# Norm blocks in pairs and a deferred attention epilogue in a hybrid mLSTM and attention block on eight cores

## The chip, the cores and the metric

The kernel runs on all eight cores of one Trainium2 chip, as one program. Two cores share one of the four sequences. A core has five engines that run side by side: PE multiplies matrices, ACT applies functions, DVE does elementwise work, POOL (GpSimd) and SP (here only issuing transfers) do little (busy shares of the kernel before, core 3: PE 69%, ACT 53%, DVE 36%, POOL 2%). They work from SBUF, the core's working memory; PE writes its products to PSUM, which this program uses as eight banks, 0 to 7. Reading a bank out is called an eviction. The metric is the device time of the slowest core, in microseconds (us), lower being better.

Executions of one kernel do not all agree: in some of them the cores of a die (one half of the chip, cores 0 to 3 or 4 to 7) show a lower granted TensorE clock, and the time is some per cent longer. The granted clock is the share of the full clock that the profile records; in these traces it is 0.5, 13/16 or 1 (2423, 588 and 3928 us on core 1 of the kernel before), and a mean of these is quoted for a stretch. Such executions are called slow and are not compared with fast ones. The medians of the kernel before lie between 6999 and 7117 us over this study, on different chips and with different shares of slow executions, so kernels are compared by ratios of fast runs to the kernel before on the same chip, and parts of a kernel by the traces.

## The reference, cut to what matters

One decoder block: a norm, two token mixers (an mLSTM and a differential attention) side by side on its result, their merge, a second norm and a gated feed-forward part.

```python
def rms_norm(x, g):
    xf = x.astype(jnp.float32)
    y = xf * lax.rsqrt(jnp.mean(xf * xf, axis=-1, keepdims=True) + RMS_EPS)
    return (y * g.astype(jnp.float32)).astype(x.dtype)
...
h = rms_norm(x, norm1_g[l]) * (1.0 + scale1) + shift1          # first norm
proj = h @ w_in[l]
...
p = jax.nn.softmax(logits, axis=-1)                            # two maps per head
wts = p[:, :, 0] - lam * p[:, :, 1]
ha = einsum(wts, v)                                            # shortened here
ha = rms_norm(ha, a_norm_g[l]...) * (1.0 - lam_init)           # the attention epilogue
y = sigmoid(g_m) * (hm @ w_branch_m[l]) + sigmoid(g_a) * (ha @ w_branch_a[l])
x = x + gate1 * (y @ w_out[l])
h2 = rms_norm(x, norm2_g[l]) * (1.0 + scale2) + shift2         # second norm
```

D_MODEL is 1024, the sequence has 8192 tokens, and there are 4 attention heads of width 128.

## The kernel before

A core works through 16 units of 512 tokens. Units 0 to 6 only build keys, values and the mLSTM state (first norm and projections). Units 7 to 15 are full: first norm, projections, attention with the mLSTM woven in, merge, second norm, feed-forward. That makes 16 first and 9 second norms, and 9 units with 4 attention heads. Unit 7 does one quarter of its queries only (32 items per head); units 8 to 15 have 74 to 130 items per head.

The program is written as a list of operations. Each goes to one engine's queue in the order in which it is emitted, and semaphores are derived from the buffers that it reads and writes. **An engine takes its queue in order**, so what is emitted first runs first on that engine. The traces show it: for ACT, the Square of the fourth norm block of unit 10 (kernel before, core 3) started at 3050.55, behind the third block's evictions, though all rows of x had landed by 3039.2 at the latest. A norm is four blocks of 128 tokens, each emitted from end to end:

```python
def norm_block(st, j, mult, shift, hdst, b_hdst, tagp):
    ...
    S.op("act", activation(out=junk, in_=xs[:, j, :], func=Square, accum_out=ss[:, 0:1]))
    S.op("act", activation(out=ss[:, 1:2], in_=ss[:, 0:1], func=Ln, bias=eps))
    S.op("act", activation(out=ss[:, 1:2], in_=ss[:, 1:2], func=Exp, scale=-0.5))
    S.op("dve", tensor_scalar(out=xn, in0=xs[:, j, :], scalar1=ss[:, 1:2], op0=mult))
    for half in range(2):
        pv = a PSUM bank
        ... 4 x S.op("pe", transpose(out=pv[:, cc], in_=xn[...]))
        ... 4 x S.op("act" if half == 0 else "dve", hdst = pv * mult + shift)   # the evictions
...
for j in range(4):
    norm_block(st, j, ...)
```

In attention an item is one key block for one or two query blocks: a score matmul into one of three PSUM banks (4 to 6, used as a ring), an exp on ACT, and the PV matmuls (the weights times the values), which run three items later into accumulators in banks 0 to 3. Every one or more items a step of the mLSTM (a Python generator, `mdrv`, with bank 7) is emitted between them. When a head's items are out, its epilogue follows on the spot:

```python
for h in range(4):
    for jq in range(4): memset(accs[jq])                        # DVE
    for idx in range(len(items) + LAG):
        if idx < len(items): emit_scores(items[idx], idx)       # PE, ACT
        if idx >= LAG: emit_pv(items[idx - LAG], idx - LAG)     # PE
        if gcount[0] % MSTEP == 0: next(mdrv, None)
    for jq in range(4):
        ... 5 small DVE operations: har[jq] = acc0/l0 - lam * acc1/l1, read from PSUM
    Square (ACT), tensor_reduce (DVE), Ln, Exp (ACT), 4 x scaling to haf (DVE)
    4 x transpose (PE) into score bank 4 + h % 3, copy to haT (DVE)
```

The softmax here doesn't subtract the row's maximum and nothing guards it: scores larger than these inputs give would overflow.

Of the kernel before, what the change touches and what calls it, by code (L numbers as in the profile page):

```python
# [188 lines left out]
def build_program(NCTX, NFULL, debug=False):  # L189
# [45 lines left out]
    with ExitStack() as top:  # L235
# [19 lines left out]
        def bfview(bank):  # L255
            return bank[:].bitcast(BF16)
# [192 lines left out]
        for u in range(NU):  # L449
# [3 lines left out]
            with ExitStack() as su:  # L453
# [23 lines left out]
                def norm_block(st, j, mult, shift, hdst, b_hdst, tagp):  # L477
# [4 lines left out]
                    if ck not in st.ncache:  # L482
# [4 lines left out]
                    S.op("act", lambda e: e.activation(out=junk[:], in_=xs[:, j, :], func=AF.Square, scale=1.0 / 32.0, accum_out=ss[:, 0:1]),  # L487
                         reads=[b_xs[j]], writes=[bl])
                    S.op("act", lambda e: e.activation(out=ss[:, 1:2], in_=ss[:, 0:1], func=AF.Ln, bias=epst[:, 0:1], scale=1.0), reads=[bl, CONST], writes=[bl])
                    S.op("act", lambda e: e.activation(out=ss[:, 1:2], in_=ss[:, 1:2], func=AF.Exp, scale=-0.5), reads=[bl], writes=[bl])  # L490
                    S.op("dve", lambda e: e.tensor_scalar(out=xn[:], in0=xs[:, j, :], scalar1=ss[:, 1:2], scalar2=None, op0=ALU.mult),
                         reads=[bl, b_xs[j]], writes=[b_xn])
                    for half in range(2):
                        pb, pbb = nbank()
                        pv = bfview(pb)[:, 0:512].rearrange("p (c t) -> p c t", c=4)
                        for cc in range(4):
                            c = half * 4 + cc
                            S.op("pe", lambda e: e.transpose(out=pv[:, cc, :], in_=xn[:, c * 128:(c + 1) * 128], identity=identb[:]),  # L498
                                 reads=[b_xn, cb[0]], writes=[pbb])
                        for cc in range(4):  # L500
# [4 lines left out]
                            else:  # L505
                                S.op("dve", lambda e: e.tensor_scalar(out=hdst[:, c, j * 128:(j + 1) * 128], in0=pv[:, cc, :], scalar1=mult[:, c:c + 1],
                                                                     scalar2=shift[:, c:c + 1], op0=ALU.mult, op1=ALU.add), reads=[pbb, CONST], writes=[b_hdst[1]])

                with ExitStack() as st:
# [13 lines left out]
                    for j in range(4):  # L523
                        norm_block(st, j, mult1, shift1, hT, (b_hT, b_hT2), "n1")
# [322 lines left out]
                if full:  # L847
                    with ExitStack() as st:
# [34 lines left out]

                        for h in range(4):
# [65 lines left out]
                            for jq in range(4):  # L950
                                ab, abb = accs[jq]
                                av = ab[:, 0:260].rearrange("p (m c) -> p m c", m=2)
                                S.op("dve", lambda e: e.tensor_scalar(out=rr[:, 2 * jq:2 * jq + 2], in0=av[:, :, 128], scalar1=1e-30, scalar2=None, op0=ALU.max), reads=[abb], writes=[b_a])  # L953
                                S.op("dve", lambda e: e.reciprocal(out=rr[:, 2 * jq:2 * jq + 2], in_=rr[:, 2 * jq:2 * jq + 2]), reads=[b_a], writes=[b_a])
                                S.op("dve", lambda e: e.tensor_tensor(out=rr[:, 2 * jq + 1:2 * jq + 2], in0=rr[:, 2 * jq + 1:2 * jq + 2], in1=neglam[:], op=ALU.mult),
                                     reads=[b_a, CONST], writes=[b_a])
                                S.op("dve", lambda e: e.tensor_scalar(out=har[:, jq, :], in0=av[:, 0, 0:128], scalar1=rr[:, 2 * jq:2 * jq + 1], scalar2=None, op0=ALU.mult),
                                     reads=[abb, b_a], writes=[b_a])
                                S.op("dve", lambda e: e.scalar_tensor_tensor(out=har[:, jq, :], in0=av[:, 1, 0:128], scalar=rr[:, 2 * jq + 1:2 * jq + 2], in1=har[:, jq, :],
                                                                            op0=ALU.mult, op1=ALU.add), reads=[abb, b_a], writes=[b_a])  # L960
                            S.op("act", lambda e: e.activation(out=hsq[:], in_=har[:], func=AF.Square, scale=1.0 / math.sqrt(128.0)), reads=[b_a], writes=[b_a])
                            S.op("dve", lambda e: e.tensor_reduce(out=hss[:, 0:4], in_=hsq[:], axis=AX.X, op=ALU.add), reads=[b_a], writes=[b_a])
                            S.op("act", lambda e: e.activation(out=hss[:, 4:8], in_=hss[:, 0:4], func=AF.Ln, bias=epst[:, 0:1], scale=1.0), reads=[b_a, CONST], writes=[b_a])
                            S.op("act", lambda e: e.activation(out=hss[:, 4:8], in_=hss[:, 4:8], func=AF.Exp, scale=-0.5), reads=[b_a], writes=[b_a])
                            for jq in range(4):
                                S.op("dve", lambda e: e.scalar_tensor_tensor(out=haf[:, jq, :], in0=har[:, jq, :], scalar=hss[:, 4 + jq:5 + jq], in1=ang[:, h * 128:(h + 1) * 128],  # L966
                                                                            op0=ALU.mult, op1=ALU.mult), reads=[b_a, CONST] + cb, writes=[b_a])
                            tb, tbb = banks[4 + h % 3], bbufs[4 + h % 3]
                            tv = bfview(tb)[:, 0:512].rearrange("p (j t) -> p j t", j=4)
                            for jq in range(4):  # L970
                                S.op("pe", lambda e: e.transpose(out=tv[:, jq, :], in_=haf[:, jq, :], identity=identb[:]), reads=[b_a, cb[0]], writes=[tbb])  # L971
# [310 lines left out]
```

## Time and profile before

The times are medians; the stage rows are read from the trace of each kernel's profiled execution, as the mean over the eight cores of the sum over all units. A stage begins and ends at the first or last matmul (or Square) that belongs to it, so the rows of one core add up to its span.

| | before |
|---|---|
| median of the first 6 runs | 6998.55 us |
| profiled run: slowest core, and all | 7048.9 us, 6953.4 to 7048.9 us |
| preamble (weights recast) | 557.3 us |
| first norms (16) | 336.9 us |
| projections | 1433.1 us |
| attention with mLSTM (9 units) | 2503.0 us |
| merge | 592.4 us |
| second norms (9) | 177.5 us |
| feed-forward | 1324.7 us |
| tail of the units | 72.9 us |

### The profile page before, as it was taken

Reading aid. Unit: us, or ns where it says so; the run is one execution under the profiler, and the core shown is the slowest. Engines: PE = TensorE matmul, PEld = TensorE weight load, DVE = VectorE, ACT = ScalarE, POOL = GpSimd, SP = SyncE. Lnnn points to the kernel's source line nnn. Section 1 sums busy time; section 2 is a strip of 40 time slices with the busy share of each in tenths; the row PEclk is TensorE's granted clock in tenths of the full one; section 3 lists DMA queues with packets and bytes.
Section 4 is the critical chain, followed back from the end, with each engine's and each line's share of the span. In section 5 each row is a group of like instructions: output and inputs, shape, how many; then the busy total and the mean of one; then the engine's idle time right before and its main releaser. Section 6 shows DMA issues by size and latency. Waiting matters only on the chain.

```text
span 7048.9 us, 96859 instructions; the slowest of 8 cores (6953.4 to 7048.9 us)
## 1 busy us (share of the span) xinstructions
PE 4834.7 (69%) x30216; PEld 2584.9 (37%) x30216; DVE 2556.0 (36%) x5233; ACT 3713.7 (53%) x8056; POOL 130.6 (2%) x196
## 2 busy tenths in 40 slices
PE   8003554557677677768777876787688768876887
PEld 6001222233243244335334532453354335433543
DVE  0002333445433532533353254215321532253225
ACT  0113343445375466448546843774486458646864
POOL 0000000000000000000000000000000000000000
PEclk8555666778788788879888987888788889988998
DMA  5995122123112312221231131222212221232122
GB/s 183 240 248 161 48 82 80 54 92 116 69 37 91 119 52 76 99 84 45 72 139 49 43 147 57 64 79 102 83 44 76 107 85 46 73 112 84 48 74 99
DMA packets 141277, 645.25 MB, mean 92 GB/s; under 512 B 20720, under 2 KB 25328, under 8 KB 96112
## 3 DMA queue, kind: packets, MB, share of 16 engines
q1 hardware_dynamic: 125424, 571.82, 24.7%
q0 software_dynamic: 15360, 67.25, 2.7%
q8 instruction: 262, 4.29, 0.2%
q14 instruction: 231, 1.89, 0.1%
HBM read 571.76 MB, written 67.24 MB: 91 GB/s over the span
## 4 chain that ended last, share of the span: by engine, by line
PE 57%; ACT 13%; DVE 10%; DMA 10%; issue 8%; DVEq 0%; SPq 0%; ACTq 0%; POOL 0%; POOLq 0%
PE bank L923 12%; PE bank L939 9%; PE bank L1076 7%; PE bank L620 6%; PE bank L1120 5%; DMA wb_scr<-s_wbo 4%; PE bank L1003 4%; PE bank L558 3%; PE bank L1017 2%; PE bank L997 2%; ACT s_pex L929 2%; PE bank L405 2%; ACT s_fu L1080 1%; ACT s_njunk L487 1%; ACT s_hT L503 1%
## 5 line engine op out<-in xcount | busy, mean ns | idle before, releaser
L929 ACT ACTIVATE s_pex<-bank,s_farb 128x512 bf16<-128x512 f32 (+1 forms) x3128 | 1843.4, 803 | 322.9 <-PE bank L923 128.6
L923 PE MATMUL bank<-s_Qbd,s_kch 128*128 128x512 bf16 (+1 forms) x3392 | 1286.5, 384 | 179.5 <-DMA s_kch<-kt_scr 123.9
L939 PE MATMUL bank<-s_vch,s_pex 128*128 128x130 bf16 x12672 | 1302.7, 224 | 4.6 <-ACT s_pex L927 2.2
L939 PEld LDWEIGHTS bank<-s_vch,s_pex 128*128 128x128 bf16 x12672 | 1012.2, 99 | 405.8 <-issue 97.5
L498 PE MATMUL bank<-s_identb,s_n1xn 128*128 128x128 bf16 x512 | 64.7, 306 | 770.1 <-DMA s_xs<-x 409.9
L1095 DVE SCALAR_TENSOR_TENSOR s_fu<-bank,s_fcw,s_fu 128x511 f32<-128x511 f32 (+1 forms) x704 | 493.6, 744 | 236.4 <-ACT s_fhalo L1088 142.7
L1076 PE MATMUL bank<-s_hT,s_pf 128*128 128x512 bf16 x2304 | 536.8, 396 | 49.6 <-DVE s_fu L1095 34.5
L923 PEld LDWEIGHTS bank<-s_Qbd,s_kch 128*128 128x128 bf16 x3392 | 337.5, 100 | 487.7 <-issue 266.6
L1120 PE MATMUL bank<-s_w_down,s_actT 128*128 128x512 bf16 x1584 | 370.3, 400 | 138.1 <-DVE s_actT L1105 138.1
L1080 ACT ACTIVATE s_fu<-bank,s_fcb,s_fcw 128x510 f32<-128x510 f32 x352 | 285.5, 811 | 275.3 <-DVE s_actT L1105 207.6
L487 ACT ACTIVATE s_njunk<-s_xs 128x1024 bf16<-128x1024 f32 x100 | 106.3, 1063 | 546.7 <-DMA s_xs<-x 474.7
L1076 PEld LDWEIGHTS bank<-s_hT,s_pf 128*128 128x128 bf16 x2304 | 230.8, 101 | 350.7 <-issue 113.6
L498 PEld LDWEIGHTS bank<-s_identb,s_n1xn 128*128 128x128 bf16 x512 | 49.5, 137 | 787.7 <-issue 787.7
L420 ACT CAST s_wbo<-s_wst 128x4096 bf16<-128x4096 f32 x16 | 57.7, 3604 | 484.6 <-DMA wb_scr<-s_wbo 300.6
L1120 PEld LDWEIGHTS bank<-s_w_down,s_actT 128*128 128x128 bf16 x1584 | 160.7, 102 | 347.8 <-issue 193.9
L503 ACT ACTIVATE s_hT<-bank,s_shift,s_mult 128x128 bf16<-128x128 bf16 x400 | 150.6, 457 | 236.1 <-PE bank L498 236.1
L1076 PE MATMUL bank<-s_hT,s_wup 128*128 128x512 bf16 x864 | 209.9, 405 | 47.5 <-ACT s_fu L1080 24.1
L953 DVE TENSOR_SCALAR s_rr<-bank 128x2 f32<-128x2 f32 x144 | 21.8, 151 | 598.3 <-PE bank L923 589.7
L971 PE MATMUL bank<-s_identb,s_haf 128*128 128x128 bf16 x144 | 21.1, 300 | 313.1 <-DVE s_haf L966 313.1
L558 PE MATMUL bank<-s_hT,s_pf 128*128 128x512 bf16 x768 | 205.2, 437 | 21.7 <-DVE s_mbc L538 11.7
L1083 ACT ACTIVATE s_fu<-bank,s_fbc,s_fcw 128x1 f32<-128x1 f32 x704 | 219.2, 383 | 0.0
L422 DVE CAST s_wbo<-s_wst 128x4096 bf16<-128x4096 f32 x16 | 36.7, 2294 | 350.0 <-DMA wb_scr<-s_wbo 304.4
(218 smaller groups left out, 6401.7 us busy)
## 6 DMA issues: line engine op xcount, KB each, us to landing
s_pf<-wb_scr SPq DMA_DIRECT2D x120, 1024.0 KB, 12.5
s_wst<-wall SPq DMA_DIRECT2D x32, 2048.0 KB, 20.7
s_vch<-va_scr SPq DMA_DIRECT2D x208, 260.0 KB, 2.7
s_kch<-kt_scr SPq DMA_DIRECT2D x208, 256.0 KB, 2.8
s_w_down<-wb_scr SPq DMA_DIRECT2D x9, 5632.0 KB, 22.4
wb_scr<-s_wbo POOLq DMA_DIRECT2D x32, 1024.0 KB, 21.2
s_xs<-x SPq DMA_DIRECT2D x64, 512.0 KB, 6.1
s_wup<-wb_scr SPq DMA_DIRECT2D x27, 1024.0 KB, 7.0
```

The costliest lines, as they stand in the source:

```text
L503: S.op("act", lambda e: e.activation(out=hdst[:, c, j * 128:(j + 1) * 128], in_=pv[:, cc, :], func=AF.Identity, scale=mult[:, c:c + 1], bi ...
L558: S.op("pe", lambda e: e.matmul(pb[:], lhsT=wv[:, dc, k * 128:(k + 1) * 128], rhs=hT[:, dc, :], start=(dc == 0), stop=(dc == 7)), reads=[w ...
L620: S.op("pe", lambda e: e.matmul(pb[:, 0:n], lhsT=hT[:, dc, tsl], rhs=wv[:, dc, :], start=(dc == 0), stop=(dc == 7)), reads=[wbf, b_hT, b_h ...
L923: S.op("pe", lambda e: e.matmul(sv, lhsT=kch[ri][:, kk * 128:(kk + 1) * 128], rhs=rhs, start=True, stop=not near), reads=[b_kch[ri], b_Qbd ...
L929: S.op("act", lambda e: e.activation(out=pex[px][:, 0:256 * nq], in_=sv, func=AF.Exp, bias=farb[:, h:h + 1], scale=1.0), reads=[spb, cb[14 ...
L939: S.op("pe", lambda e: e.matmul(ab[:, m * 130:(m + 1) * 130], lhsT=pex[px][:, c0:c0 + 128], rhs=vch[ri][:, kk, :], start=False, stop=False ...
L1003: S.op("pe", lambda e: e.matmul(pg[:], lhsT=gv[:, dc, (c % 4) * 128:(c % 4 + 1) * 128], rhs=hT[:, dc, :], start=(dc == 0), stop=(dc == 7)) ...
L1076: S.op("pe", lambda e: e.matmul(pb[:], lhsT=wv[:, dc, k * 128:(k + 1) * 128], rhs=h2T[:, dc, :], start=(dc == 0), stop=(dc == 7)), reads=[ ...
L1080: S.op("act", lambda e: e.activation(out=uu[kk_][:, m0:512], in_=pb[:, m0:512], func=AF.Identity, scale=wsel[:, q, 2:3], bias=fcb[:, q:q + ...
L1083: S.op("act", lambda e: e.activation(out=uu[kk_][:, col:col + 1], in_=pb[:, col:col + 1], func=AF.Identity, scale=wsel[:, q, 2:3], bias=fb ...
L1095: S.op("dve", lambda e: e.scalar_tensor_tensor(out=uu[kk_][:, sh:512], in0=pb[:, 0:512 - sh], scalar=wsel[:, q, tp:tp + 1], in1=uu[kk_][:, ...
L1120: S.op("pe", lambda e: e.matmul(po[:], lhsT=actT[:, f, tsl], rhs=wdv[:, f, n * 512:(n + 1) * 512], start=(f == 0), stop=(f == NF - 1)), re ...
```

## The change

Its intent is to overlap engines in two places where they took turns. Norm blocks become generators that pause after each stage and are run in pairs. The attention epilogue becomes a generator too: its first step copies the four accumulators to SBUF at the head's end, which frees the banks, and the remaining steps are emitted inside the next head, one per six items.

```diff
-                    S.op("act", activation(out=junk[:], in_=xs[:, j, :], func=AF.Square, ...))
+                    S.op("act", activation(out=xn[:], in_=xs[:, j, :], func=AF.Square, ...))
+                    yield
                     S.op("act", Ln ...); S.op("act", Exp ...)
+                    yield
                     S.op("dve", xn = xs * ss ...)
+                    yield
                     (transposes of both halves)
+                    yield
                     (evictions of both halves)
+                    yield
+                def run_norms(st, mult, shift, hdst, b_hdst, tagp):
+                    for pair_ in ((0, 1), (2, 3)):
+                        alive_ = [norm_block(st, j_, ...) for j_ in pair_]
+                        (one step of each in turn, until both have ended)
...
+                        def attn_epi(h, accs):
+                            for jq in range(4):
+                                S.op("dve", tensor_copy(out=aS[:, jq], in_=accs[jq]))   # 128 x 260
+                            yield
+                            for jq in range(4):
+                                (the same five DVE operations, from aS)
+                                yield
+                            S.op("act", Square)
+                            yield
+                            S.op("dve", tensor_reduce)
+                            yield
+                            S.op("act", Ln); S.op("act", Exp)
+                            yield
+                            4 x S.op("dve", scaling to haf)
+                            yield
+                            4 x S.op("pe", transpose into bank 4 + h % 3); S.op("dve", copy to haT)
+                            yield
...
                                 if gcount[0] % MSTEP == 0:
                                     next(mdrv, None)
-                            (the epilogue)
+                                if idx % 6 == 5:
+                                    next(epi[0], None)
+                            for _ in epi[0]:
+                                pass                      # steps left over
+                            epi[0] = attn_epi(h, accs)
+                            next(epi[0], None)            # the copies
+                        for _ in epi[0]:
+                            pass                          # the last head: all at once
```

## The prediction

> **What bounds the kernel now.** I read the overview first, then the chain that ended last, then the costliest groups, and last the timeline of one norm and one head boundary, because the change touches only those two places.
>
> ```profile
> PE 4834.7 (69%) x30216; PEld 2584.9 (37%) x30216; DVE 2556.0 (36%) x5233; ACT 3713.7 (53%) x8056; POOL 130.6 (2%) x196
> ...
> PE 57%; ACT 13%; DVE 10%; DMA 10%; issue 8%; DVEq 0%; SPq 0%; ACTq 0%; POOL 0%; POOLq 0%
> ...
> L498 PE MATMUL bank<-s_identb,s_n1xn 128*128 128x128 bf16 x512 | 64.7, 306 | 770.1 <-DMA s_xs<-x 409.9
> L971 PE MATMUL bank<-s_identb,s_haf 128*128 128x128 bf16 x144 | 21.1, 300 | 313.1 <-DVE s_haf L966 313.1
> ```
>
> No engine is full. PE carries 57% of the chain, but ACT and DVE carry 23%, and much of that is serial work in which PE has nothing. The last two rows say where: the norm transposes (L498) and the epilogue transposes (L971). The 313.1 us of L971 belongs to 36 boundaries (4 heads in each of 9 units with attention), 8.7 us each. Of the 770.1 us, 410 us is one wait for the weight preamble and not the norm.
>
> The timeline at one head boundary (unit 10, heads 0 and 1; start, duration, what):
>
> ```profile
> 3209.79 0.60 PE L939 MATMUL bank<-s_vch,s_pex 128*128 128x130 bf16 x6
> ...
> 3216.52 0.35 DVE L959 SCALAR_TENSOR_TENSOR s_har<-bank,s_rr,s_har 128x128 f32<-128x128 f32 x1
> 3216.96 0.63 ACT L961 ACTIVATE s_ahsq<-s_har 128x512 f32<-128x512 f32 x1 [6.99 <-DVE s_har L959]
> 3217.69 0.69 DVE L962 TENSOR_REDUCE s_ahss<-s_ahsq 128x4 f32<-128x512 f32 x1 [0.82 <-ACT s_ahsq L961]
> 3218.47 0.30 ACT L963 ACTIVATE s_ahss<-s_ahss,s_epst 128x4 f32<-128x4 f32 x1 [0.88 <-DVE s_ahss L962]
> 3218.86 0.21 ACT L964 ACTIVATE s_ahss<-s_ahss 128x4 f32<-128x4 f32 x1
> 3219.17 1.72 DVE L966 SCALAR_TENSOR_TENSOR s_haf<-s_har,s_ahss,s_ang 128x128 bf16<-128x128 f32 x4 [0.79 <-ACT s_ahss L964]
> 3221.03 0.59 PE L971 MATMUL bank<-s_identb,s_haf 128*128 128x128 bf16 x4 [10.64 <-DVE s_haf L966]
> ...
> 3222.29 1.44 PE L923 MATMUL bank<-s_Qbd,s_kch 128*128 128x512 bf16 x3 [0.68 <-DVE s_haT L972]
> 3222.97 2.42 ACT L929 ACTIVATE s_pex<-bank,s_farb 128x512 bf16<-128x512 f32 x4 [3.91 <-PE bank L923]
> ```
>
> After the last PV matmul ends at 3210.39, DVE and ACT hand small pieces to each other until 3221; PE runs the next score only at 3222.29. The gap is 11.9 us, and ACT does 1.1 us of work in it. Between boundaries ACT is the limit: it was busy 47.08 of 49 us from 3223 to 3272, one 512-wide exp every 0.58 us, while PE needs 0.44 us per item.
>
> One of the four norm blocks of unit 10:
>
> ```profile
> 3045.57 1.06 ACT L487 ACTIVATE s_njunk<-s_xs 128x1024 bf16<-128x1024 f32 x1
> 3046.52 0.21 ACT L487 ACTIVATION_READ_ACCUMULATOR s_njunk<-s_xs 128x1 f32 x1
> 3046.82 0.29 ACT L489 ACTIVATE s_n1ss<-s_n1ss,s_epst 128x1 f32<-128x1 f32 x1
> 3047.21 0.20 ACT L490 ACTIVATE s_n1ss<-s_n1ss 128x1 f32<-128x1 f32 x1
> 3047.59 0.76 DVE L491 TENSOR_SCALAR s_n1xn<-s_xs,s_n1ss 128x1024 bf16<-128x1024 f32 x1 [1.86 <-ACT s_n1ss L490]
> ...
> 3048.49 1.01 PE L498 MATMUL bank<-s_identb,s_n1xn 128*128 128x128 bf16 x8 [3.97 <-DVE s_n1xn L491]
> 3049.17 1.50 ACT L503 ACTIVATE s_hT<-bank,s_shift,s_mult 128x128 bf16<-128x128 bf16 x4 [1.76 <-PE bank L498]
> ...
> 3050.55 1.06 ACT L487 ACTIVATE s_njunk<-s_xs 128x1024 bf16<-128x1024 f32 x1
> ```
>
> The next block's Square starts when this block's evictions have issued: a period of 4.98 us, in which ACT waits 1.76 us and PE does only the transposes. The four blocks stand alone in the trace, some 20 us per norm; 25 norms run (16 first, 9 second).
>
> [...] Square of block j+1 needs nothing of block j, its rows had landed, and it still starts behind the evictions. So emission order is what counts. [...] no table load stands in the boundary above, so moving Square, Ln and Exp in between the attention's exps adds none. [...] the granted clock was 0.50 from 3034 to 3056, 0.57 from 3210 to 3222 and 0.98 from 3223 to 3272. [...]
>
> **The change, part by part: norms.** Blocks now go in pairs: both Squares, both Ln/Exp, both scalings, the transposes, then the evictions. Work is the same (the sum of squares just writes its unused output into the block's own tile). ACT's own work per block is 4.98 - 1.76 = 3.22 us. In a pair the second Ln/Exp (0.69 us) lies inside the first block's wait, which leaves 1.76 - 0.69 = 1.07 us. The pair is then 2 x 3.22 + 1.07 = 7.5 us against 9.96: 2.45 us saved.
> First norm, units 0 to 7: two pairs, 4.9 us, times 8 = 39 us. Units 8 to 15: the first pair also has a table load (1.28 us), so block 1's Square stood 6.25 us after block 0's, and the pair took 11.2 us. Its second piece of x lands 1.4 us after the first, a delay of some 0.3 us for the pair: 7.5 + 1.28 + 0.3 = 9.1, saving 2.1 us; with the second pair 4.6 us, times 8 = 37 us.
> Second norm: Square, Ln and Exp of block 0 already run under the output projection. Now block 1's do too. From the first scaling (3487.58) to the end of block 1's evictions (3495.57) it was 8.0 us; now 1.58 us to the first eviction and two evictions of 1.5: 4.6 us. Saving 3.4 + 2.45 = 5.85 us, times 9 = 53 us.
> Norms together: **about 128 us**, all of it with PE waiting, so on the path.
>
> **The change: attention epilogue.** At the end of a head four copies (128x260) empty the accumulators into SBUF and the rest runs as steps inside the next head, one per 6 items. The same copy in the mLSTM part (L790) takes 0.43 us, the clearing memset 0.28. Three copies can go before the last PV matmul, so copy and two memsets end some 1.2 us after it. The first PV of the next head needs about as long, for its score and exp. I count no wait here.
> Removed: the time from the last PV to the first score. I measured it at the 24 boundaries inside units 8 to 15: 7.9 to 12.6 us, sum 235 us. In unit 7 the three gaps sum to 33 us, but its heads have only 32 items, so about half of the steps are drained at the end, some 3.5 us: gain 22 us. The last head of each unit is drained as before: gain 0, minus some 0.6 us for the copies, times 9 = -5 us.
> Given back: Square, Ln and Exp (1.1 us plus a wait between the last two, 1.25 us) now run while ACT is the limit: 24 x 1.25 = 30 us. The transposes take a score bank in the middle of the ring: PE must wait for ACT to empty it, and for DVE to copy before the bank is used again, an estimated bubble of 1 us for ACT: 24 us. In units 8 and 9 mLSTM steps come every one or two items and share DVE with 8 us of epilogue per head: I take 15 us in all. [...]
> Sum: 235 + 22 - 5 - 30 - 24 - 15 + 5 = **188 us**.
>
> Together 128 + 188 = 316 us. The unprofiled median is 6998.55, so **6682 us**, 4.5% less.
>
> **The rivals.** (1) The deferred steps stall the stream they are put into. PE keeps matmuls in order, so a transpose or an mLSTM matmul behind a late DVE piece stops the scores. For: mLSTM waits of 0.3 to 1 us stand in the PE timeline already. Against: six items are 3.5 us, and each step has one or two pieces. If each of ten steps cost 0.7 us, 24 heads would lose 170 us, the attention gain would be near zero: about 6850 us.
> (2) The gain comes back through the clock. Core 3 ran at 13/16 for 597 us, core 5 for 15. With fewer pauses the first die may be held there more often. Against: attention is limited by ACT, and PE at 13/16 needs 0.54 us per item, still under 0.58. The projections and the feed-forward part are as dense as before. I give it up to 40 us: 6720.
> (3) The norm gain is hidden, since weights or x land later anyway. For: 6 MB of loads run during the first norm. Against: x had landed about 5 us after its first piece, the last weight at 3049, before its use. If true in units 8 to 15, the result is 6720.
> (4) The stalls I subtracted are absorbed by the slack between PE and ACT: 6640.
>
> **Range and chances.** (4) bounds it below; (2) and (3) together, or half of (1), above: 6620 to 6770. Less than 2% faster needs more than 6859, so all of (1). Faster 0.96, same 0.035, slower 0.005.
>
> **What would show it.** Right: the epilogue transposes' idle time falls from 313 us to under 120; last PV to first score falls from 8-12 us to under 1.5 at the inner boundaries; the norm lasts about 15 us instead of 20, with two Squares side by side; ACT busy stays within 2%. Wrong: exps in mid-head that wait 1 us or more at each step, new DVE waits of mLSTM matmuls, a lower clock in the attention windows, or Squares that wait for x.

The passages cut above are statements that were not read from the traces, and a remark and a term of the sum that rested on them: an estimated credit of 5 us. With that term the attention sum came to the 188 us that the prediction gives and the total to 6682 us; without it the sum is 235 + 22 - 5 - 30 - 24 - 15 = 183 us and the total some 6687 us. The 24 us for the bank and the 15 us for DVE are estimates. So is the 0.54 us per item at 13/16, from the 0.44 us: on core 1 of the kernel before, back-to-back PV matmuls of L939 started 67 ns apart at 13/16 and 56 ns at full clock, and 128x512 matmuls of L1076 263 and 216 ns.

## More of the kernel before

Beside the views that the prediction shows, one is worth a look: the table of PE's waits on core 1. Its columns are what PE was about to do, what ended the wait, the sum of the waits in us, how often, and the longest.

```profile
PE bank L498 <- DVE s_n1xn L491: 748.2, 64, 385.1
PE bank L971 <- DVE s_haf L966: 313.4, 36, 11.3
...
PE bank L498 <- DVE s_n2xn L491: 128.8, 36, 4.1
...
PE bank L923 <- ACT s_pex L929: 37.7, 93, 1.3
```

PE waits at 64 first-norm transposes (16 norms of 4 blocks; one wait of 385 us is the preamble), at 36 epilogue transposes and at 36 second-norm transposes. The last row is the wait of a score matmul for an exp to empty its bank: within the heads it is short but frequent. To the change, the first three rows are what might go, and the last is where the price would show.

## The result

| | before | after |
|---|---|---|
| median, with lowest and highest | 7011.45 us (6981.11 to 7125.79, 20 runs) | 6691.45 us (6659.46 to 6837.22, 10 runs) |
| profiled run: slowest core, and all | 7048.9 us, 6953.4 to 7048.9 us | 6723.5 us, 6622.3 to 6723.5 us |
| clock, median of die 0 and of die 1 | 0.813, 0.828 | 0.837, 0.848 |
| ratio of fast runs | | 0.9529, 95% interval 0.9491 to 0.9566 |

A ratio is the mean time of one kernel's fast runs over that of the other's in the same rounds, so it isn't quite the ratio of the medians quoted. Both profiled runs are fast ones. The change made the kernel 4.7% faster.

The stages of the traces, summed as above, show where:

| stage | before | after | difference | predicted |
|---|---|---|---|---|
| first norms | 336.9 | 258.7 | -78.2 | -76 |
| second norms | 177.5 | 121.0 | -56.5 | -53 |
| attention | 2503.0 | 2312.2 | -190.8 | -188 |
| projections | 1433.1 | 1429.6 | -3.5 | 0 |
| merge | 592.4 | 590.1 | -2.3 | 0 |
| feed-forward | 1324.7 | 1327.3 | +2.6 | 0 |

The three lines of the page of the kernel after that answer to those shown of before are the overview of the engines, the chain that ended last, and the group of the first norm's transposes:

```profile
PE 4784.6 (71%) x30216; PEld 2571.4 (38%) x30216; DVE 2587.8 (38%) x5377; ACT 3695.0 (55%) x8056; POOL 130.6 (2%) x196
...
PE 57%; ACT 14%; DMA 11%; issue 9%; DVE 9%; SPq 0%; DVEq 0%; POOL 0%; ACTq 0%; POOLq 0%
...
L503 PE MATMUL bank<-s_identb,s_n1xn 128*128 128x128 bf16 x512 | 59.7, 309 | 692.9 <-DMA s_xs<-x 416.4
```

The work is the same: the counts of PE and ACT instructions have not moved, DVE has 144 more (four copies at each of 36 heads), ACT's busy time is 0.5% lower, and its table loads are 68 on core 1 in both. The chain's shares have hardly moved either. They are averages over stages, and tell nothing of what the change did. The epilogue transposes have left the page's list of costly groups. PE's waits on core 1 tell it:

```profile
PE bank L503 <- DMA s_xs<-x: 416.4, 1, 416.4
PE bank L503 <- DVE s_n1xn L493: 276.6, 31, 14.7
...
PE bank L946 <- DVE s_haf_1 L940: 101.2, 10, 12.4
...
PE bank L503 <- DVE s_n2xn L493: 71.9, 18, 5.7
PE bank L990 <- ACT s_pex L996: 67.0, 147, 2.4
...
PE bank L946 <- ACT s_pex L996: 12.6, 15, 1.1
```

There are half as many waits of norm transposes, for there is one per pair. The epilogue's wait for its scaling fell from 313.4 to 101.2 us in ten waits, nine of them at the last head of a unit, where nothing follows to hide it (3.7 us more stand in a row of the other tile set). The price is in the two rows of `s_pex`: score matmuls wait 67.0 us for exps in place of 37.7, and 15 of the epilogue's transposes wait 0.8 us each for an exp to empty a score bank.

One boundary, in the timeline of core 1 (unit 12, heads 2 and 3; start, duration, what):

```profile
4425.38 1.06 PE L1006 MATMUL bank<-s_vch,s_pex 128*128 128x130 bf16 x8
...
4426.30 0.81 PE L990 MATMUL bank<-s_Qbd,s_kch 128*128 128x512 bf16 x3
...
4426.55 0.43 DVE L919 COPY s_accS<-bank 128x260 f32<-128x260 f32 x1 [0.23 <-PE bank L1006]
4426.77 4.16 ACT L996 ACTIVATE s_pex<-bank,s_farb 128x512 bf16<-128x512 f32 x7 [0.74 <-PE bank L990]
4427.03 1.11 DVE L954 MEMSET bank<- 128x260 f32 x4
```

The next head's scores start at 4426.30, before the modelled end of the last PV matmul at 4426.44; at the boundary that the prediction shows they came 11.9 us after it. ACT stands still 0.74 us at this boundary. The last of the four copies and the clearing run beside the first scores. One norm of unit 10 on core 1:

```profile
2904.49 1.06 ACT L487 ACTIVATE s_n1xn<-s_xs 128x1024 bf16<-128x1024 f32 x1 [50.33 <-DMA s_xs<-x]
...
2905.75 1.06 ACT L487 ACTIVATE s_n1xn<-s_xs 128x1024 bf16<-128x1024 f32 x1
...
2906.92 1.28 ACT L490 ACT_TABLE_LOAD   x1
2908.21 0.29 ACT L490 ACTIVATE s_n1ss<-s_n1ss,s_epst 128x1 f32<-128x1 f32 x1
...
2910.56 2.90 ACT L511 ACTIVATE s_hT<-bank,s_shift,s_mult 128x128 bf16<-128x128 bf16 x8 [1.28 <-PE bank L503]
...
2913.32 1.09 ACT L487 ACTIVATE s_n1xn<-s_xs 128x1024 bf16<-128x1024 f32 x1
```

Two Squares stand side by side, then one wait of 1.28 us serves both blocks, then eight evictions in a row. The first pair's period is 2913.32 - 2904.49 = 8.8 us, where the prediction had 9.1.

### The profile page after: what moved, and what is told of

It reads as the page before. It is cut to its first block, busy times and chain, and to the rows that moved or that the text cites. A ratio compares the mean times of both kernels' runs of the same rounds, so it can differ in the third digit from the quotient of the medians.

```text
span 6723.5 us, 97071 instructions; the slowest of 8 cores (6622.3 to 6723.5 us)
## 1 busy us (share of the span) xinstructions
PE 4784.6 (71%) x30216; PEld 2571.4 (38%) x30216; DVE 2587.8 (38%) x5377; ACT 3695.0 (55%) x8056; POOL 130.6 (2%) x196
## 4 chain that ended last, share of the span: by engine, by line
PE 57%; ACT 14%; DMA 11%; issue 9%; DVE 9%; SPq 0%; DVEq 0%; POOL 0%; ACTq 0%; POOLq 0%
PE bank L990 12%; PE bank L1006 9%; PE bank L1127 7%; PE bank L641 7%; PE bank L1171 5%; DMA s_wst<-wall 5%; PE bank L1055 4%; ACT s_pex L996 3%; PE bank L579 2%; PE bank L1069 2%; PE bank L1049 2%; ACT s_fu L1131 2%; PE bank L405 2%; PE bank L749 1%; DMA s_xs<-x 1%
## 5 line engine op out<-in xcount | busy, mean ns | idle before, releaser
L990 PE MATMUL bank<-s_Qbd,s_kch 128*128 128x512 bf16 (+1 forms) x3392 | 1262.8, 376 | 206.6 <-DMA s_kch<-kt_scr 122.4
L1146 DVE SCALAR_TENSOR_TENSOR s_fu<-bank,s_fcw,s_fu 128x511 f32<-128x511 f32 (+1 forms) x704 | 493.6, 744 | 242.0 <-ACT s_fhalo L1139 162.0
L487 ACT ACTIVATE s_n1xn<-s_xs 128x1024 bf16<-128x1024 f32 x64 | 67.8, 1073 | 476.5 <-DMA s_xs<-x 476.4
L919 DVE COPY s_accS<-bank 128x260 f32<-128x260 f32 x144 | 56.7, 424 | 318.3 <-PE bank L990 303.6
L595 DVE SCALAR_TENSOR_TENSOR s_acc<-bank,s_mcw,s_acc 128x511 f32<-128x511 f32 (+2 forms) x192 | 131.8, 742 | 84.1 <-PE bank L579 43.8
## 6 DMA issues: line engine op xcount, KB each, us to landing
s_w_down<-wb_scr SPq DMA_DIRECT2D x9, 5632.0 KB, 21.6
```

What stands on the lines that cost most here:

```text
L990: S.op("pe", lambda e: e.matmul(sv, lhsT=kch[ri][:, kk * 128:(kk + 1) * 128], rhs=rhs, start=True, stop=not near), reads=[b_kch[ri], b_Qbd ...
L1146: S.op("dve", lambda e: e.scalar_tensor_tensor(out=uu[kk_][:, sh:512], in0=pb[:, 0:512 - sh], scalar=wsel[:, q, tp:tp + 1], in1=uu[kk_][:, ...
```

## The experiments

Twelve kernels ran in three batches, each batch on one chip with runs of the kernel before. In batch one to three its medians were 7062.2, 7113.68 and 7116.55 us, so the times of different batches are not compared. The sums by stage come from the traces, as in the tables above, and "attention" is the sum over nine units. How far such a sum can be trusted is seen from kernels that share the code of a stage, in fast profiles: attention is 2503.0 and 2499.0 us with the old epilogue (before, e1) and 2310.0 to 2315.4 with the new one (after, e2, e8, e10), but the merge, untouched until e11, spreads from 578.9 to 592.4. For kernels of more than one edit the diffs are against the kernel after.

**The theory** after the first reading was the prediction's: each removed gap sat on the path, and what comes back in the heads is ACT's moved work and the disturbed ring of score banks. **Its rivals**: the clock gives or takes part of it; the two halves of the change help or hinder each other; the steps stall the stream; and, for the last heads and unit 7, the copies and the drained steps cost more than was reckoned.

### Each half alone

The first kernel has the new norms with the old epilogue, the second the old norms with the new epilogue.

```diff
 # e1_norms_only
-                        (attn_epi and its steps)
+                        (the epilogue of the kernel before)
 # e2_epilogue_only
-                    run_norms(st, mult1, shift1, hT, (b_hT, b_hT2), "n1")
+                    for j in range(4):
+                        norm_block(st, j, mult1, shift1, hT, (b_hT, b_hT2), "n1")   # the old block, also for n2
```

> Only the paired norms, with the old epilogue. Theory (the two parts are separate places on the path and add up): first norms 259 us and second norms 121 us per core as in the changed kernel, attention 2503 us as before, in all about 131 to 135 us less than before (ratio 0.981). Rival (the norm gain comes back elsewhere, for example as longer waits for weights in the stages after it): norms shorter but less than 100 us left in the time.

> Only the deferred epilogue, with the old norms. Theory: attention falls from 2503 to about 2312 us, all other stages as before, so about 190 us less than before (ratio 0.973). Rival (denser attention lowers the granted clock of the projections and the feed-forward part): those stages grow by over 10 us per core and less than 170 us is left.

| | first norms | second norms | attention | median | ratio to before |
|---|---|---|---|---|---|
| before | 336.9 | 177.5 | 2503.0 | 7062.2 | 1 |
| e1_norms_only | 257.6 | 121.2 | 2499.0 | 6875.6 (5 runs) | 0.9758, 0.9684 to 0.9831 |
| e2_epilogue_only | 336.4 | 177.9 | 2310.0 | 6943.45 (4 runs) | too few fast runs |
| after | 258.7 | 121.0 | 2312.2 | | |

Each half moves its own stages by what it moves them in the whole change, to within 4 us, and leaves the other's where they were. So the halves add up, and neither needs the other. The timed ratio of e1 holds the expected value in its interval, but the interval spans 1.5%, wider than what is to be settled; the four runs of e2, between 6807.68 and 7048.78 us, gave no ratio.

### The last head without copies

```diff
-                            for jq in range(4):
+                            last = h == 3
+                            for jq in range(0 if last else 4):
                                 (copy to aS)
...
-                                av = aS[:, jq, :, :]
+                                av = accs[jq][0][...] if last else aS[:, jq, :, :]    # read PSUM
```

> The changed kernel, but the last head of each unit, which nothing follows, works from PSUM without the four copies, as before. Theory: in the changed kernel the pieces of the first three query blocks could no longer start before the last PV matmul, because all four copies stand ahead of them on DVE; that is the 3.0 us by which the last drain grew (9.7 to 12.7 us in the trace). So each of the units 8 to 15 gets 3 us back, 24 us in attention, about 0.4% of the time. Rival (the drain grew because its SBUF pieces or the copies themselves are slow): copies alone are 1.4 us, so at most 12 us come back.

Attention fell from 2312.2 to 2284.1 us, by 28.1 (26.6 of it in units 8 to 15); the ratio to before was 0.9446 (0.9383 to 0.951, 5 runs). The timelines of the drain on core 1 in unit 11, first of the kernel after, where the last score ends at 3860.66:

```profile
3862.31 0.17 DVE L923 TENSOR_SCALAR s_rr_1<-s_accS 128x2 f32<-128x2 f32 x1
...
3872.41 0.58 PE L946 MATMUL bank<-s_identb,s_haf_1 128*128 128x128 bf16 x4 [10.74 <-DVE s_haf_1 L940]
```

and of this experiment, where it ends at 3762.12:

```profile
3761.74 0.35 DVE L929 TENSOR_SCALAR s_har<-bank,s_rr 128x128 f32<-128x128 f32 x1 [0.46 <-DVE s_rr L927]
...
3771.23 0.59 PE L948 MATMUL bank<-s_identb,s_haf 128*128 128x128 bf16 x4 [8.10 <-DVE s_haf L942]
```

With the copies, the arithmetic of the first query block starts 1.65 us after the last score. Without them that block is already under way before the last score: its accumulator was complete, and only the copies of the others stood in front of it in DVE's queue. The transposes come 11.75 us after the last score with the copies and 9.11 us without. From the start of the last score to the transposes' end it is 9.6 to 9.8 us in units 8 to 15 of the kernel before, 12.6 to 13.0 after, and 9.6 to 10.0 here.

### All the steps at once

```diff
-                                if idx % 6 == 5:
-                                    next(epi[0], None)
+                                if idx == 5:
+                                    for _ in epi[0]:
+                                        pass
```

> The changed kernel, but the whole deferred epilogue is issued in one lump after the sixth item of the next head, not in steps. Theory (the steps are what hides it: PE keeps its order, so the transposes in one lump make PE wait for the whole chain of 8 to 9 us): PE waits some 7 us at each of 27 inner boundaries, attention rises from 2312 to about 2490 us, the gain of the deferral is nearly gone, time about 6860 us. Rival (freeing the accumulators by the copies is what counts, and the stream's own slack hides the rest): attention stays within 30 us of 2312.

Attention went to 2540.7 us, 51 above the expected value: 228 more than with spread steps, and 38 more than before the change; the ratio to before was 0.9828 (0.9776 to 0.9879, 4 runs), close to the 0.9758 of the norms alone. PE's waits for `haf` were 346.5 us at 36 places on core 1, 9.6 us each where 7 were expected. So it is not the deferral that pays but the spreading: a transpose that PE meets while DVE and ACT are still at work on its input holds the scores behind it. The first rival of the prediction, steps that stall the stream, is real where the steps come too close; in the kernel after they are far enough apart, for units 8 to 15.

### ACT's share doubled, and removed

The first of these does the epilogue's Square, Ln and Exp twice (same result). The second moves them off ACT, with DVE operations in their place (a reciprocal where a reciprocal square root belongs). Its output is wrong, which doesn't matter for the time.

```diff
 # e5_double_act: each of the three operations once more
+                            S.op("act", activation(out=hsq[:], in_=har[:], func=AF.Square, ...))
...
+                            S.op("act", Ln ...); S.op("act", Exp ...)
 # e9_no_act
-                            S.op("act", activation(out=hsq[:], in_=har[:], func=AF.Square, ...))
+                            S.op("dve", tensor_tensor(out=hsq[:], in0=har[:], in1=har[:], op=ALU.mult))
...
-                            S.op("act", Ln ...); S.op("act", Exp ...)
+                            S.op("dve", tensor_scalar(... mult, add eps)); S.op("dve", reciprocal)
```

> The changed kernel with the epilogue's Square, Ln and Exp on ACT each issued twice (the pair of Ln and Exp is repeated, so the second Ln overwrites the result with the same value). Theory (inside a head ACT is the limit, and what moved there costs its full time): the heads that carry the steps grow by about 1.25 us each, 24 heads in units 8 to 15, so 30 us for those, plus 1.25 us at each of the 9 drains, 11 us: attention 2312 to about 2353 us. Rival (slack between PE and ACT absorbs it): only the 11 us of the drains appear.

> The changed kernel with nothing of the epilogue on ACT: Square becomes a product on DVE, and Ln and Exp become a scaling and a reciprocal on DVE, which gives a wrong result on purpose (1/x where 1/sqrt(x) is wanted). It settles what ACT's moved work costs inside the heads, since the two earlier runs do not add up: heads of units 8 to 15 grew by 27 us in all, moving the transposes to another bank took 19 us off, and doubling ACT's part added 41 us (with drains). Theory A (ACT's moved work costs its full 1.25 us per head, and something else was won in the heads): attention 2312 to about 2282 us. Theory B (the transposes make 19 of the 27 us, ACT's single part the remaining 8): attention falls by 8 to 12 us only.

The profile of e5 fell in the slow state of die 1 (clock near 0.80), so only die 0 is read (clocks 0.843 to 0.853): attention 2359.5 us against 2314.2 on die 0 of the kernel after, 45.3 more, where 41 was expected. Its ratio of fast runs was 0.9559 (0.944 to 0.9678, 6 runs). Work added to ACT inside a head is paid in full here.

In e9 attention was 2289.1 us: 23.1 less than after, 21.6 of it in units 8 to 15. The first theory expected about 30 and the second 8 to 12, so neither number was met; the first is nearer. Work taken from ACT gives back some two thirds of its time. Four runs gave a median of 6790.99 us and no ratio. A reading that fits both is that ACT is the limit during most of a head but not all of it. That is argued and not shown; where in a head the cost arises is shown in the table by items further down.

### More steps, for unit 7

```diff
-                                if idx % 6 == 5:
+                                if idx % 3 == 2:
```

> The changed kernel with one epilogue step every 3 items, not 6, so that all steps fit into the 32-item heads of unit 7. Theory (unit 7 gained only 6 us, where 22 were predicted, because steps remain at the end of its heads and drain there): its head boundaries fall from 14 to about 4 us in sum and the last drain from 17 to about 13 us, so unit 7 gains some 14 us; units 8 to 15 change by under 10 us in sum. Rival (unit 7 is slow because its mLSTM matmuls wait behind the epilogue on DVE): its heads, 28.5 us each, grow by what the boundaries lose, and unit 7 stays at about 142 us.

Unit 7 fell from 142.3 to 130.7 us, and units 8 to 15 together changed by 9 us upward, about 1 us each. The ratio was 0.9487 (0.9393 to 0.9581, 4 runs). One boundary of unit 7 in the timeline of the kernel after, core 1, at the end of the third head:

```profile
1478.25 0.38 PE L946 MATMUL bank<-s_identb,s_haf_1 128*128 128x128 bf16 x4 [1.96 <-DVE s_haf_1 L940]
...
1482.39 2.05 PE L783 MATMUL bank<-s_RL,s_ones_f 128*128 128x512 f32 x2 [2.81 <-DVE s_Kw L762]
...
1486.46 0.47 ACT L996 ACTIVATE s_pex<-bank,s_farb 128x256 bf16<-128x256 f32 x1 [6.31 <-PE bank L990]
```

With 32 items a head has room for five of the nine steps that follow the copies. The rest is emitted together at the head's end; PE waits 1.96 us for the scaling. Then the four copies and the four memsets of the next boundary stand in DVE's queue ahead of an mLSTM operation, PE waits 2.81 us for that one, and with the four fp32 matmuls (1482.39 to 1486.14, 3.75 us) ACT gets no score for 6.31 us. Most of that last wait is no doing of the change, for ACT waits 5.33 us at the same place of the kernel before (at 1510.45 on core 1).

A sum over unit 7 tells more (mean of the six cores whose traces hold every score; cores 2 and 4 lack some). The gaps are counted from the start of a last score to the next head's first, the end from the start of the last score of all to the end of the transposes.

| unit 7 | four heads | three gaps | end | sum |
|---|---|---|---|---|
| before | 101.9 | 38.3 | 7.7 | 148.0 |
| after | 110.8 | 14.2 | 17.3 | 142.3 |
| e6_step_3 | 109.6 | 8.2 | 12.7 | 130.5 |

The change took 24.1 us of gaps away, but the heads grew by 8.9 and the end by 9.6, where the third head's left-over steps are drained in front of the last head's own. A step every three items leaves none to drain: it shortened gaps and end by 6.0 and 4.6 us and the heads by only 1.2.

### The transposes out of the ring

```diff
-                            tb, tbb = banks[4 + h % 3], bbufs[4 + h % 3]
+                            tb, tbb = banks[7], bbufs[7]
```

> The changed kernel with the epilogue's transposes in the PSUM bank of the mLSTM part, not in a bank of the score ring. Theory after the result: the bubble of 1 us per head that was predicted for the bank does not exist (heads of units 8 to 15 grew by 27 us in sum, and ACT's moved work alone makes 30), so attention stays within 8 us of 2312. Rival (the prediction's term): up to 24 us less.

This kernel's result was wrong (relative error 0.047), which was not meant: by the program, the mLSTM keeps live data in bank 7 over its pauses, and the transposes write over it. Its instruction counts are those of the kernel after and its busy times agree within 1% (PE 4755.2 and 4784.6 us), so its time may still be read. Attention was 2293.5 us, 18.7 less, all of it in units 8 to 15. My revised theory had expected a change within 8 us, and it missed; the prediction's own term of 24 us for the bank's bubble was the better one. Four runs gave a median of 6751.65 us and no ratio.

### All four norm blocks together, and skewed

```diff
 # e8_norm_four: tiles for four blocks, all in step
-                    for pair_ in ((0, 1), (2, 3)):
+                    for pair_ in ((0, 1, 2, 3),):
 # e10_norm_skew: Square and Ln/Exp by pairs, the later stages by fours
+                    gens_ = [norm_block(st, j_, ...) for j_ in range(4)]
+                    for pair_ in ((0, 1), (2, 3)):
+                        for step_ in range(2):
+                            for j_ in pair_:
+                                next(gens_[j_])
+                    for step_ in range(4):
+                        for g_ in gens_:
+                            next(g_, None)
```

> The changed kernel with all four norm blocks interleaved at once, not in pairs (two more tiles for the normalised rows). Theory (inside a pair ACT is nearly the limit, 6.44 of 7.5 us, and only the wait at the seam of the pairs is left): the first norms fall by about 2 us each (32 us in sum, 259 to 227), the second norms, whose Squares all run under the output projection, by about 4 us each (37 us, 121 to 84); time about 65 us less than the changed kernel, ratio to before about 0.944. Rival (with four blocks ahead, Squares wait for rows of x that land up to 5 us after the first): first norms no shorter than in pairs.

> Four norm blocks again, but Square, Ln and Exp of blocks 0 and 1 are issued before those of 2 and 3, and all scalings, transposes and evictions after. Theory (in the run with four at once the second norm gained only 7 us in sum because Ln of block 0 stood in ACT's queue behind Square of block 3, which waits for the last row of the output projection, and behind the table load): now only the last two Squares wait for it, second norms 121 to about 85 us in sum, first norms about 230 us as with four at once; about 65 us less than the changed kernel. Rival (DVE, which scales and evicts, is the limit of the second norm): second norms stay above 105 us.

| | first norms | second norms | ratio |
|---|---|---|---|
| after (pairs) | 258.7 | 121.0 | 0.9529, 0.9491 to 0.9566 |
| e8_norm_four | 230.2 | 113.7 | 0.9461, 0.932 to 0.9603 (4 runs) |
| e10_norm_skew | 211.6 | 88.8 | none (6 runs, median 6748.98) |

In e8 the first norms gained 28.5 us, near what was expected, and the second norms only 7.3 of 37. ACT's timeline in e8 (core 0, unit 15, second norm) says why:

```profile
6468.41 1.06 ACT L487 ACTIVATE s_n2xn<-s_xs 128x1024 bf16<-128x1024 f32 x1 [2.30 <-DVE s_xs L1072]
...
6469.58 1.28 ACT L490 ACT_TABLE_LOAD   x1
6470.88 0.29 ACT L490 ACTIVATE s_n2ss<-s_n2ss,s_epst 128x1 f32<-128x1 f32 x1
```

The first line is the Square of the fourth block, which waits for the last row of the output projection. The Ln of the first block, whose Square was done at 6459.2, stands behind it in ACT's queue, and so does the table load. "Four in step" put the earliest block behind the latest input. The skewed order lets the first pair's Ln and Exp go before the second pair's Squares. PE's waits for the second norm's blocks on core 1, in nine units, are in e8

```profile
PE bank L503 <- DVE s_n2xn L493: 51.7, 9, 5.7
```

and in e10

```profile
PE bank L503 <- DVE s_n2xn L493: 21.7, 9, 2.4
```

(The third block's tile has another name here; its waits in the second norms are 3.5 us more in e10 and none in e8.) The same work in another order saves some 3 us in each second norm, and the order of e10 beats the change's own pairs by 47.1 + 32.2 = 79 us in the sums of the stages.

### Two weights of the merge earlier

While reading the merge I saw PE wait for two of its weights at each unit's start, and had them loaded during attention, into space that single instead of double epilogue tiles set free.

```diff
+                    wearly = {nm_: (sbt(sw, "we_" + nm_, [128, 4096], BF16), ...) for nm_ in ("ba", "ga0")}
...
-                            p = h % 2
+                            p = 0
...
+                            if h in (1, 2):     # at the start of heads 1 and 2
+                                S.dma("sp", wearly[nm_][0][:], wb_d[:, off_:off_ + n_], ...)
```

> The changed kernel, with two of the weights of the merge stage loaded during heads 1 and 2 of the attention (the room comes from tiles that the change left unused and from single instead of double epilogue tiles). In the chain of waits of both kernels PE waits some 8 us for one of these loads after the barrier at the end of each attention stage. Theory: the merge stage loses 7 to 8 us in each of 9 units, 590 to about 522 us, attention is as before (2312), so this is worth 1.0% of the time. Rival (the next weight in the queue takes the place of the wait): the merge stage falls by less than 30 us.

The profile fell in the slow state of die 0, so die 1 is read: the merge took 554.2 us in nine units against 583.5 on die 1 of the kernel after, 29 less and not the 68 expected; attention was 2308.3 against 2310.3, so one set of epilogue tiles is enough. The ratio was 0.9529 (0.9436 to 0.9621, 6 runs), that of the kernel after, and too wide to show 29 us. The estimate took a piece of the chain for a wait: in unit 14 of the kernel after, core 5, the chain has 8.50 us for the load of `s_w_ga`, but PE had other matmuls for most of them. PE's own waits there are

```profile
PE bank L1049 <- DMA s_w_ba<-wb_scr: 2.0, 1, 2.0
PE bank L1055 <- DMA s_w_ga<-wb_scr: 1.2, 1, 1.2
```

That is 3.2 us in this unit. Over the nine units these two waits sum to 14 to 25 us on the four cores of die 1, and the stage fell by 26 to 36 us there, so they cover some two thirds of it; the rest is not traced.

### All that helped

The last kernel has e3's direct last head, a step every three items in unit 7 alone, Square on DVE, the skewed norms and the early weights.

```diff
+                                if idx % 6 == 5 or (u == NCTX and idx % 3 == 2):
-                            S.op("act", activation(out=hsq[:], in_=har[:], func=AF.Square, ...))
+                            S.op("dve", tensor_tensor(out=hsq[:], in0=har[:], in1=har[:], op=ALU.mult))
 (with the edits of e3, e10 and e11)
```

> What helped, together: last head without copies (-28 us of attention), steps every 3 items in unit 7 (-12), Square of the epilogue on DVE (about -13), skewed norms (-65), merge weights early (-68). If they add up: about 186 us less than the changed kernel per core in the trace (6669 to about 6483), ratio to before about 0.926 by the timed runs. If the parts share waits, for example if the early weights delay the K and V loads, attention stays above 2270 us and the ratio above 0.935.

| stage | after | e12_all | difference |
|---|---|---|---|
| first norms | 258.7 | 211.4 | -47.3 |
| second norms | 121.0 | 89.0 | -32.0 |
| attention | 2312.2 | 2261.9 | -50.3 |
| merge | 590.1 | 556.0 | -34.1 |
| sum of all stages | 6668.9 | 6506.9 | -162.0 |

The result is correct, with a median of 6649.07 us (6530.44 to 6790.45, 6 runs) on a chip where the kernel before took 7116.55, and a ratio of 0.9303 (0.9214 to 0.9391). That interval lies below the one of the kernel after, so **this version is faster than the change**, and the sum of its stages is the least of all. The sum was expected at 6483 us, 24 us less than measured; about 34 of the 68 us expected in the merge failed to come, as in e11. In attention, e3 and e6 alone account for 28.1 and 11.6 us of the 50.3; the remaining 10.6 us are put down to the Square by subtraction (no run isolates it), 0.63 us at 24 inner boundaries or 15 us at face value, and so two thirds of it again.

## Why the prediction was right

The total was predicted at 6682 us and came out at 6691.45. The three sums by stage were each met within 4 us. But a sum can be met by errors that cancel, and in the attention part that is what happened: its mechanism was right, and that its total came within 3 us was luck. Core 3's trace, units 8 to 15, gives the terms (a head is timed from its first to its last score):

| term of the attention sum | predicted | measured | by |
|---|---|---|---|
| inner gaps removed, units 8 to 15 | 235 | 235.9 | gaps 272.7 to 36.8 us, core 3 |
| unit 7 | 22 | 6 | 148.2 to 142.3 us, all cores |
| copies at the last heads | -5 | -24 to -27 | 8 x 3.0 us; e3, units 8 to 15 |
| growth of the heads, net | -64 | -27 to -32 | 2004.5 to 2031.3 us, core 3; core 1 |

- **Norms.** Right step by step: pairs that share one wait, a longer first pair where the table load stands in it (16.9 us for a norm of units 8 to 15 against 15.5 in units 0 to 7, all cores), and a second norm whose second block now also runs ahead. It was 13.4 us from 19.7, 6.3 saved where 5.85 was said. The third rival, a gain hidden behind loads, found no support.
- **Inner gaps.** Right. At the boundary shown there is neither a gap nor a wait of ACT beyond 0.74 us, and the term was measured, not guessed.
- **Copies at the last heads: mis-sized**, in the step "minus some 0.6 us for the copies". It is 3.0 us each. The 0.6 counted the copy that comes last; it forgot that all four stand in DVE's queue ahead of arithmetic that in the kernel before had started on the finished accumulators. e3 took the term back whole.
- **Unit 7: mis-sized**, and not in the step "some 3.5 us" for the drained steps of each boundary: the gaps lost 24.1 us, a little more than the 22 predicted. What the sum left out is that the heads grew by 8.9 us, by the table under e6, and the last head's end by 9.6, so the gain shrank to 6. Of these 9.6 us the copies make 1.7 (e3: 15.6 us for 17.3) and the left-over steps 4.6 (e6); the rest is open. Of the 8.9 us, 3.7 stand in the first three items of the three inner heads, behind copies and memsets, and the rest further on, among the steps. e6 brought 11.6 of the missing 16 back.
- **Growth of the heads: mis-sized.** The prediction had 30 for ACT, 24 for the bank, 15 for DVE and, as a credit, 5. e9 gives 21.6 for ACT and e7 18.7 for the bank. These alone add up to 40, while the heads grew by 27 to 32, and the traces show where the rest comes from.

For the 24 inner heads of units 8 to 15, the time from a head's first score to each later one can be compared with the kernel before. The Square is emitted after item 29 (counted from 0), Ln and Exp after 41, the transposes after 53. The change in each stretch of a head, in us, as the mean of cores 1, 3, 5 and 7, is

| | items 0 to 6 | 6 to 24 | 24 to 36 (Square) | 36 to 48 (Ln, Exp) | 48 to 60 (transposes) | whole head |
|---|---|---|---|---|---|---|
| after | -0.73 | +0.15 | +0.44 | +0.47 | +0.80 | +1.14 |
| e9_no_act | -0.75 | +0.15 | -0.01 | -0.01 | +0.81 | +0.23 |
| e7_bank_7 | -0.71 | +0.15 | +0.43 | +0.47 | +0.08 | +0.42 |

ACT's part costs 0.91 us a head, 24 x 0.91 = 22 us; the bank 0.80, or 19 us; DVE's four arithmetic steps, which lie before item 24, at most 0.15, or 4 us. None of the costs changes when another is removed. The credit is 0.73 us a head, or 18 us where 5 were predicted, and it falls in the first six items, before any step that PE or ACT takes part in. The clock may have a part in it: at the first score of an inner head the granted clock was one half in all 144 cases of the kernel before (six cores), for another 4.5 us on the mean, and in none of the kernel after. The half clock came 0.3 to 4.9 us after a head's last PV matmul (median 3.0). But in the kernel before an early score also had to wait for the copy to `haT` (0.68 us at the boundary that the prediction shows), and no run separates the two: **what part of the 18 us is the clock stays open**.

The errors of -16 (unit 7), of -19 to -22 (copies) and of +32 to +37 (growth) cancel to a few us.

Of the rivals, (1), stalled steps, is refuted for the change as written, and shown as a real danger by e4. (2), the clock, is refuted: projections and feed-forward differ by 3.5 us or less in sum, and attention fell by 192.0 us on the first die, which ran at 13/16 of the clock for 518 to 597 us in either trace, and by 189.5 on the second, where that time was 15 to 26 us. (That the time at 13/16 did not rise, core 1 having 588 us before and 541 after, would alone show little: among the fast profiles it lies between 0 and 1130 us on core 3.) (3) is refuted by the norm sums. (4), full absorption, is refuted by e5.

The signs that the prediction named came as said: the wait before the epilogue's transposes is under 120 us (101.2, and 117.5 with the two smaller rows), norms take 15 to 17 us with two Squares side by side, and ACT's busy time is within 2%.

## What to carry to other kernels

Where engines take turns on a chain of small pieces, emit the pieces inside a stretch that another engine limits, with room for each piece to finish before an in-order engine meets the next one: spread steps gained 191 us here, and the same steps in one lump lost 38. Size the places where nothing follows separately (last head, short units), for there a copy that frees a buffer only stands in front of the work. And when blocks are interleaved, no stage of an early block should be queued behind a late block's input; the order, not the number of blocks in flight, decided e8 against e10.

## What the traces show of table loads, sums and the clock

- The table load takes 1.28 us here, and ACT hardly stands still around it: in the norm of the kernel after the second Square's last piece ends at 2906.91, the load starts at 2906.92, and Ln starts at 2908.21, 0.01 us after its end. All 33 loads of core 1 that follow other work of ACT at once look so (17 to 19 ns before the load, 11 or 12 ns after it). A switch cost 1.3 us here.
- Each Square with a sum is followed here by a second ACT instruction (ACTIVATION_READ_ACCUMULATOR) of 0.19 to 0.24 us; Squares that have nothing to wait for follow each other at 1.04 us (2913.32 and 2914.36 in the kernel after).
- The clock that this kernel, with its pauses, got on all cores differs from run to run. With PE busy for 71% of the span, core 1 of the kernel after was at 13/16 for 541 us of 6723.5 and at full clock for 4043; no core of e12_all, with PE busy for 72% of the slowest core's span, was ever at 13/16 in its profiled run (mean clocks 0.853 to 0.857), and core 3 of e10_norm_skew was for 1130 us in a fast one (mean clock 0.824).
